# The MLP's second product by seven products of half-size blocks, in a hybrid decoder step on one core

## The chip, the cores and the metric

The kernel runs on one core of one Trainium2 chip. The metric is the device time of one execution in microseconds (us); lower is better. Engines are named as in the profile: PE does matmuls, PEld loads their stationary operands, DVE and ACT are the vector and the scalar engine, POOL is GpSimd, SP issues most transfers.

## The reference

One inference step of a one-layer decoder on 2048 prompt tokens (model width 1024) and 8 x 8 sample tokens: a shared input projection; forgetting attention (FoX) over the prompt and, for the sample tokens, over 8192 cached positions in pages; an mLSTM recurrence; an output projection with layer norm; and a squared-ReLU MLP with a second layer norm. All data are float32. The part that matters here is the end:

```python
mix = jnp.concatenate([fox_h, mn], axis=-1) @ w_o
x1 = _layer_norm(DN_ALPHA * x + mix, ln1_g, ln1_b)
hid = jnp.square(jax.nn.relu(x1 @ w1))             # 1024 -> 4096
return _layer_norm(DN_ALPHA * x1 + hid @ w2, ln2_g, ln2_b)   # 4096 -> 1024
```

## The kernel before

Each product of float32 operands is made of three matmuls on split operands: ACT rounds an operand to the matmul's reduced form ("hi", `split_hi`, L153), DVE subtracts that from the original ("lo", `split_lo`, L156), and `mm3` (L161 to L163) issues hi x hi, hi x lo and lo x hi into one PSUM bank.

The program has stages: the input projection with the mLSTM, the prompt attention (`phase_b`), the output projection with the first norm (`phase_o`), and the MLP (`phase_c`). The attention of the sample tokens over their cached pages is a Python generator of 294 steps. `tick(us)` counts the work that has been emitted and calls the next step (`attend`) each time `PACE_C` = 5 more has gone by in the last two stages. A step loads, scores or weighs: gathers of keys (`k_gather`, L1479, tile `kT`) and of values (`v_gather`, L1590, tiles `vt`, or `xr` and `vx` while `vx["more"]` allows a second place) are issued from POOL; `qk_step` (tile `sQ`) and `pv_step` (tile `sO`, L1614) are their matmuls. `take_back` runs steps until the second place is empty again.

`phase_c` goes over four blocks of tokens, `CB`: three of four tiles of 128, and a last one with the 64 sample rows added as tile 16 (576 columns). Within a block there are 16 groups of 256 hidden features:

- `hidden(fc)`: two weight tiles of `w1` (`piece`: one 512 KB load into `wr`, split into `wh` and `wl`), then for each 128 features a PSUM bank `ph` of 8 x 3 matmuls (moving operand 512 tokens wide, or twice 288 in the last block), Relu and Square on ACT into `hq`, and the split into `hh` and `hl`.
- `output([fc])`: two weight tiles of `w2`; for each token tile and each half of the 1024 output columns a bank `py` of 2 x 3 matmuls with 512 columns, which DVE adds into the row tile `y` (L1305; at the first group L1303 also multiplies by alpha). The last two groups share one call, `output([14, 15])`; after each tile's last addition there stands `layer_norm` (statistics, the power on POOL at L173, scaling on ACT at L175, gain on DVE at L176, bias on POOL at L177, or on DVE in the last block) and the store.

The order is `hidden(fc)`, then `output([fc - 1])`. Before the last `output` of a block, the next block's normed rows are loaded and turned by PE transposes into the operands `x1h` and `x1l` (`load`, `x1_turn`). In the third block, after group 13, the remaining attention steps are run, and `sampled()` does the output projection and first norm of the sample rows and stores them, to be read back as tile 16. The framework's scheduler orders each engine's instructions by the order of emission and a simulated readiness, so matmuls of `hidden` and `output` are found interleaved on PE.

## Time and profile before

| | |
|---|---|
| median of 3 runs | 3358.97 us (3357.42 to 3363.64) |
| the profiled execution | 3354.03 us; its span 3352.3 us, granted PE clock 0.986 |
| busy share of the span | PE 96%, DVE 56%, ACT 41%, POOL 26% |
| the MLP's first and last matmul | at 1607.0 us and 3338.2 us of the span |
| second-product matmuls | 3 x 1088 with 512 columns (of them 3 x 64 for the 64 sample rows) |

The span goes from the first to the last instruction on the core; the profiled execution's own time has 1.7 us around it. Times in rows of the trace count from the span's start. A group row gives the source line, engine, operation, output and input with their shapes, the number of instructions, their busy time, the mean duration of one in ns, and the idle time before them with what ended it. PE's matmuls overlap at their ends, so the distance between starts is the price of one, not its duration.

### The profile page before, as it was taken

The numbers are of one execution on the slowest core, as the hardware profiler recorded it, in microseconds if no ns is written. First come the engines' busy times: TensorE is split into PE (matmuls) and PEld (weight loads), VectorE is DVE, ScalarE is ACT, GpSimd is POOL, SyncE is SP. The second block draws the span as 40 slices with busy tenths as digits, with TensorE's granted clock in tenths as the row PEclk, the third lists the DMA queues.
The fourth block names the chain that finished last, engine by engine and source line by source line (L and its number), as shares of the span: only waits on it lengthen the run. The fifth ranks groups of instructions, "written<-read, shape, count | busy, mean of one in ns | idle before, by whom it ended". The sixth has DMA issues, their size and how long they took to land.

```text
span 3352.3 us, 58232 instructions
## 1 busy us (share of the span) xinstructions
PE 3225.8 (96%) x22065; PEld 2635.4 (79%) x22065; DVE 1890.9 (56%) x4781; ACT 1364.1 (41%) x2795; POOL 877.3 (26%) x925
## 2 busy tenths in 40 slices
PE   8999999998979999899999999999999999999998
PEld 8998998887857667677777777777777777888887
DVE  6857565455377878444544455445554545645545
ACT  4333343333278888422332333233433423433332
POOL 0031242332322222365322234323252110100000
PEclk9999999999989999999999999999999999999999
DMA  5575766767662322586876768767677554532221
GB/s 182 151 221 186 232 219 217 251 202 243 187 197 74 108 83 58 212 292 238 287 246 244 243 222 320 264 226 276 215 287 286 176 169 152 167 120 79 88 76 66
DMA packets 316000, 650.48 MB, mean 194 GB/s; under 512 B 61000, under 2 KB 175048, under 8 KB 314824
## 3 DMA queue, kind: packets, MB, share of 16 engines
q1 hardware_dynamic: 239032, 367.55, 35.1%
q0 software_dynamic: 74304, 270.57, 22.1%
q10 hardware_dynamic: 2384, 8.65, 0.7%
q8 instruction: 174, 2.85, 0.3%
q14 instruction: 106, 0.87, 0.1%
HBM read 593.82 MB, written 52.83 MB: 193 GB/s over the span
## 4 chain that ended last, share of the span: by engine, by line
PE 47%; DMA 4%; DVE 1%; POOL 1%; issue 1%; ACT 1%; SPq 0%; ACTq 0%; POOLq 0%; DVEq 0%
PE py L161 7%; PE py L162 7%; PE py L163 7%; PE ph L161 6%; PE ph L163 6%; PE ph L162 6%; PE sO L1614 3%; PE sQ L1502 2%; DMA wr<-w 2%; DMA vt<-cache_v,idxV 1%; PE sT L1571 1%; DMA kT<-cache_k,idxK 1%; DVE wl L156 0%; DMA vx<-cache_v,idxV 0%; PE pw L162 0%
## 5 line engine op out<-in xcount | busy, mean ns | idle before, releaser
L1305 DVE TENSOR_TENSOR y<-y,py 128x512 f32<-128x512 f32 (+1 forms) x476 | 326.2, 686 | 380.6 <-PE py L163 374.8
L153 ACT ACTIVATE wh<-wr 128x1024 fp32r<-128x1024 f32 x268 | 277.7, 1056 | 501.5 <-PE py L163 307.4
L161 PE MATMUL ph<-x1h,wh 128*128 128x512 f32 (+1 forms) x1280 | 455.1, 356 | 4.3 <-ACT wh L153 3.8
L162 PE MATMUL ph<-x1l,wh 128*128 128x512 f32 (+1 forms) x1280 | 453.6, 354 | 0.0
L163 PE MATMUL ph<-x1h,wl 128*128 128x512 f32 (+1 forms) x1280 | 451.4, 353 | 0.2 <-DVE wl L156 0.2
L161 PE MATMUL py<-wh,hh 128*128 128x512 f32 (+1 forms) x1088 | 432.6, 398 | 3.6 <-DVE y L1303 3.6
L1479 POOL DMA_INDIRECT kT<-cache_k,idxK x256 | 262.5, 1025 | 658.1 <-PE sQ L1502 596.0
L162 PE MATMUL py<-wl,hh 128*128 128x512 f32 (+1 forms) x1088 | 427.2, 393 | 0.7 <-DVE wl L156 0.7
L156 DVE TENSOR_TENSOR wl<-wr,wh 128x1024 fp32r<-128x1024 f32 x268 | 336.6, 1259 | 160.2 <-PE ph L163 82.1
L163 PE MATMUL py<-wh,hl 128*128 128x512 f32 (+1 forms) x1088 | 425.8, 392 | 0.0
L161 PE MATMUL pm<-xh,whi 128*128 128x256 f32 (+1 forms) x1024 | 302.4, 295 | 0.0
L162 PE MATMUL pm<-xl,whi 128*128 128x256 f32 (+1 forms) x1024 | 298.1, 291 | 0.0
L163 PE MATMUL pm<-xh,wlo 128*128 128x256 f32 (+1 forms) x1024 | 297.0, 290 | 0.0
L161 PEld LDWEIGHTS ph<-x1h,wh 128*128 128x128 f32 x1280 | 241.3, 189 | 45.7 <-issue 7.0
L163 PEld LDWEIGHTS ph<-x1h,wl 128*128 128x128 f32 x1280 | 241.2, 188 | 35.5 <-issue 2.1
L162 PEld LDWEIGHTS ph<-x1l,wh 128*128 128x128 f32 x1280 | 241.3, 188 | 34.6 <-issue 1.6
L161 PEld LDWEIGHTS py<-wh,hh 128*128 128x128 f32 (+1 forms) x1088 | 200.9, 185 | 60.6 <-issue 14.0
L161 PE MATMUL pm<-whi,xh 128*128 128x256 f32 (+2 forms) x816 | 237.6, 292 | 9.2 <-ACT whi L153 9.0
L1590 POOL DMA_INDIRECT vt<-cache_v,idxV x158 | 162.1, 1026 | 314.5 <-PE sO L1614 249.1
L163 PEld LDWEIGHTS py<-wh,hl 128*128 128x128 f32 (+1 forms) x1088 | 200.9, 185 | 49.5 <-issue 2.5
L162 PEld LDWEIGHTS py<-wl,hh 128*128 128x128 f32 (+1 forms) x1088 | 201.0, 185 | 41.6 <-issue 1.6
L162 PE MATMUL pm<-wlo,xh 128*128 128x256 f32 (+2 forms) x816 | 232.9, 286 | 0.6 <-DVE wlo L156 0.6
(349 smaller groups left out, 6549.8 us busy)
## 6 DMA issues: line engine op xcount, KB each, us to landing
wr<-w SPq DMA_DIRECT2D x256, 512.0 KB
wra<-w_in SPq DMA_DIRECT2D x104, 512.0 KB
Rb<-dR SPq DMA_DIRECT2D x128, 128.0 KB
xn<-xp_t SPq DMA_DIRECT2D x16, 512.0 KB
kn<-k_prompt SPq DMA_DIRECT2D x64, 128.0 KB
qn<-dq SPq DMA_DIRECT2D x128, 64.0 KB
wr<-w_o SPq DMA_DIRECT2D x16, 512.0 KB
xr<-dmix SPq DMA_DIRECT2D x16, 512.0 KB
```

The source lines that it names most:

```text
L153: last["ACT"] = A.activation(dst, src, AF.Copy, scale=scale)
L156: r = (eng or V).tensor_tensor(dst, src, hi.bitcast(F32), op=OP.subtract)
L161: T.matmul(ps, wh, xh, start=first, stop=False)
L162: T.matmul(ps, wh, xl, start=False, stop=False)
L163: last["PE"] = T.matmul(ps, wl, xh, start=False, stop=stop)
L1305: V.tensor_tensor(y, y, ps, op=OP.add)
L1479: G.indirect_dma_start(out=piece(n), out_offset=None, in_=ck, in_offset=IO(ap=idxK[:, b, j // 2, j % 2:j % 2 + 1], axis=0))
L1502: r = T.matmul(pq[h4 * 32:h4 * 32 + 32, hg].rearrange("p (k c) -> p k c", k=2), z["qb"][:, hd], kv, start=(db == 0), stop=(db == 1), skip_ ...
L1571: T.transpose(p[:, f], z["U"][u][:, hg, f].rearrange("p k t -> p (k t)"), ident)
L1590: G.indirect_dma_start(out=vt.rearrange("p f c -> p (f c)"), out_offset=None, in_=cv, in_offset=IO(ap=idxV[:, b, (kt % 4) * 4 + kt // 4, f ...
L1614: after_ = T.matmul(po[r:r + 32], z["PT"][:, hg, 2 * f + g, pg].rearrange("p h q -> p (h q)"), vts[f][:, g, hg * 256:(hg + 1) * 256], star ...
```

## The change

The 4096 hidden features are taken as two halves, and group `p` of the first half is worked together with group `p` of the second. One call of `output(p)` multiplies the block's four token tiles by 512 rows of `w2`. Both operands are cut in 2 x 2: tokens (two tiles each) by features (`a11`, `a12`, `a21`, `a22`), features by columns (`b11`, `b12`, `b21`, `b22`). In place of eight block products it does seven, in Winograd's variant of Strassen's form. Two of them are plain (a11 b11 and a12 b21, done first); the five others use sums of blocks, written in place: four of activations (`s`, `a21`, `a11`, `s` again) on DVE, four of weights (`b11`, `b12`, `b11`, `b11`) on POOL. Two PSUM banks (`X`) and two more (`Z`) go on accumulating after DVE has added their state so far into an output block, so there are 14 additions into `y` per call. Each of the seven operands is split only after its sum (`made`), two products ahead of its use. The 64 sample rows of the last block are multiplied plainly, beside those products whose weights fit (`extra`).

Around it: `hidden(p, half)` leaves its result unsplit in one of three `hq` tiles. `hidden(p + 1, 0)` is emitted before `output(p)` and `hidden(p + 1, 1)` after it. The host lays `w2` out by blocks. The next block's tokens are turned one by one between the products of the last `output`; two of their loads are issued before it. Norm statistics are taken per half row as soon as that half is complete (`norm_stats`), and in the last block the rest of the norm and the store go by halves on DVE (`norm_end`). Buffers: `wr` 5 for 4, `wh` 4 for 5, `hh` and `hl` 3 of [128, 2, 256] for 4 of 576 columns, `ph` 2 banks for 3, `py` 4 for 3; `jp` shares a buffer, and the scratch for POOL's transfer descriptors is set to 8192. Cut to its core:

```diff
-    def mm3(ps, wh, wl, xh, xl, first, stop):
+    def mm3(ps, wh, wl, xh, xl, first, stop, shared=False):
...
+    def norm_end(x, np_, st, g, b, wk, out, quick):
+        mv = wk.tile([128, 2], F32, name="ln_m2", bufs=2)
+        V.bn_aggr(mv[:np_], st[:np_])
+        rs = wk.tile([128, 3], F32, name="ln_r2", bufs=2)
+        V.tensor_scalar(rs[:np_, 0:1], mv[:np_, 1:2], EPS, None, op0=OP.add)
+        G.tensor_tensor(rs[:np_, 1:2], rs[:np_, 0:1], nhalf[:np_, 0:1], op=OP.pow)
+        if not quick:
...
+        h = [slice(i * 512, i * 512 + 512) for i in range(2)]
+        for i, e in ((0, SY), (1, A)):
+            V.scalar_tensor_tensor(x[:, h[i]], x[:, h[i]], mv[:np_, 0:1], g[:np_, h[i]], op0=OP.subtract, op1=OP.mult)
+        for i, e in ((0, SY), (1, A)):
+            V.scalar_tensor_tensor(x[:, h[i]], x[:, h[i]], rs[:np_, 1:2], b[:np_, h[i]], op0=OP.mult, op1=OP.add)
+            e.dma_start(out[:, h[i]], x[:, h[i]])
...
-        return pcw.tile([128, 1024], F32, name="wr", bufs=4)
+        return pcw.tile([128, 1024], F32, name="wr", bufs=5)
...
-        wh = C["pc"].tile([128, 1024], F32R, name="wh", bufs=5).rearrange("p (k c) -> p k c", k=k)
+        wh = C["pc"].tile([128, 1024], F32R, name="wh", bufs=4).rearrange("p (k c) -> p k c", k=k)
...
+            sums = {(0, 0): 2, (0, 1): 2, (1, 0): 1, (1, 1): 2, (2, 0): 2, (2, 1): 3}
...
+            def output(p, begun=None):
+                f1, f2 = H.pop((p, 0)), H.pop((p, 1))
+                a11, a21, a12, a22 = f1[:, :, 0:256], f1[:, :, 256:512], f2[:, :, 0:256], f2[:, :, 256:512]
+                b21, b22, b12, b11 = (raw() for _ in range(4))
+                for q, b in ((2, b21), (3, b22), (1, b12), (0, b11)):
+                    SY.dma_start(b, I["w2"][p, q])
+                s = ph.tile([128, 2, 256], F32, name="s", bufs=1)
...
+                def made(n):
+                    v = lambda o, x, y, op: V.tensor_tensor(o, x, y, op=op)
+                    g = lambda o, x, y: G.tensor_tensor(o, x, y, op=OP.subtract)
+                    w = lambda b: piece(None, b.rearrange("p (k c) -> p k c", k=2))
+                    if n == 1:
+                        r = split(a12), w(b21)
+                    elif n == 0:
+                        v(s, a21, a22, OP.add)
+                        r = split(a11), w(b11)
+                        v(a21, a11, a21, OP.subtract)
+                        v(a11, s, a11, OP.subtract)
+                        g(b11, b12, b11)
+                        g(b12, b22, b12)
+                    elif n == 2:
+                        r = split(s), w(b11)
+                        v(s, a12, a11, OP.subtract)
+                        g(b11, b22, b11)
+                    elif n == 3:
+                        r = split(a11), w(b11)
+                        g(b11, b21, b11)
+                    else:
+                        r = (split((s, a21, a22)[n - 4]), w((b22, b12, b11)[n - 4]))
+                    return r
...
+                plan = [(0, "X", True, False, 0, 0), (1, "Y", True, True, 0, 0), (3, "X", False, False, 0, 1), (2, "Z", True, False, 2, 1),
+                        (4, "Z", False, True, 0, 1), (5, "X", False, False, 2, 1), (6, "X", False, True, 2, 0)]
+                extra = {0: (0, (0, 1)), 1: (1, (0,)), 2: (0, (1,)), 4: (1, (1,))}
+                for at_, (n, kind, first_, last_, r0, half) in enumerate(plan):
+                    if at_ + 2 < 7:
+                        ops.append(made(at_ + 2))
+                    (h, l), (wh, wl) = ops[n]
+                    for i in range(2):
...
+                        for k in range(2):
+                            mm3(ps, h[:, k, c], l[:, k, c], wh[:, k], wl[:, k], first_ and k == 0, last_ and k == 1, True)
+                        add(blk[r0 + i], half, ps)
+                        tick(1.28)
...
+                    if begun and at_ in (0, 1, 3, 4):
+                        turn(ci + 1, (0, 1, 3, 4).index(at_), begun)
...
+            hidden(0, 0)
+            hidden(0, 1)
+            for p in range(8):
+                if p < 7:
+                    hidden(p + 1, 0)
+                if p == 6:
                     vx["more"] = None
...
+                output(p, begun if p == 7 and ci < 3 else None)
+                if p == 6 and ci < 3:
                     take_back()
+                    begun = [x1_load(t) for t in CB[ci + 1][:2]]
+                if p < 7:
+                    hidden(p + 1, 1)
+                if p == 6 and ci == 2:
                     while acc[1] is not None:
                         tick(100.0)
                     sampled()
```

## The prediction

> **What bounds the kernel now.** I read the page's busy shares first, then busy time by stretch of the second half (the MLP runs from about 1607 us to the end), then PE's instructions in order of time, PE's waits, and last DVE's and POOL's groups.

> ```profile
> span 3352.3 us, 58232 instructions
> PE 3225.8 (96%) x22065; PEld 2635.4 (79%) x22065; DVE 1890.9 (56%) x4781; ACT 1364.1 (41%) x2795; POOL 877.3 (26%) x925
> core 0: us, PE busy (x) PEld busy (x) DVE busy (x) ACT busy (x) POOL busy (x), PEclk, DMA share, GB/s
> 2060.00:2445.00 385.00, 379.16 (x2414) 286.72 (x2412) 185.14 (x382) 128.32 (x216) 128.53 (x129) 1.00 0.71 255
> 2890.00:2915.00 25.00, 24.82 (x128) 20.11 (x127) 19.39 (x34) 8.63 (x12) 7.31 (x5) 1.00 0.28 102
> 2915.00:2960.00 45.00, 43.97 (x286) 40.30 (x286) 26.59 (x36) 21.90 (x38) 6.37 (x4) 1.00 0.60 205
> 2960.00:3300.00 340.00, 340.00 (x2009) 301.84 (x2009) 169.77 (x231) 116.86 (x206) 0.00 (x0) 1.00 0.27 81
> PE py L161 <- DVE y L1303: 3.2, 1, 3.2
> PE sO L1614 <- DMA vt<-cache_v,idxV: 1.8, 1, 1.8
> PE sQ L1502 <- DMA kT<-cache_k,idxK: 0.8, 1, 0.8
> ```

> In the second block of tokens (2060 to 2445) PE is busy 379.16 of 385 us at full clock; its three waits there make up the 5.8 that are missing. In the last block (2960 to 3300) it never idles. DVE is at 48 to 50%, ACT at 33 to 34%, POOL at 33% and then nothing. So this stage lasts as long as its matmuls, and a matmul taken out of it is worth its own pitch, as long as the three other engines still deliver in time. A busy PE is not by itself proof of matmuls at full rate, so the pitch comes from the order of time: the first and the last of twelve consecutive second-product matmuls (128x512), nothing between them.

> ```profile
> L161 PE MATMUL py<-wh,hh 128*128 128x512 f32 x1024 | 407.7, 399 | 3.6 <-DVE y L1303 3.6
> 2460.28 0.39 PE L161 MATMUL py<-wh,hh 128*128 128x512 f32 x1
> ...
> 2462.78 0.39 PE L163 MATMUL py<-wh,hl 128*128 128x512 f32 x1
> ```

> Eleven steps in 2.50 us are 0.2273 us each. The group row's 399 ns is the time of one with its drain, which the next one overlaps; it is not the price.

> **The matmuls removed.** Before, two feature groups (a "pair" from here on) cost, per block of four token tiles, 2 groups x 4 tiles x 2 halves x 2 contraction steps x 3 = 96 matmuls. The new `output(p)` has seven products x 2 tiles x 2 x 3 = 84. The 64 sample rows of the last block cost 24 per pair either way (`extra` has four entries of six). So 12 go per pair, 8 pairs x 4 blocks = 32 pairs: 384, an eighth of the 3072 that the row's x1024 times three forms gives. 384 x 0.2273 = 87.3 us off PE. The first product is untouched.

> **What is added, engine by engine.**

> ```profile
> L1305 DVE TENSOR_TENSOR y<-y,py 128x512 f32<-128x512 f32 x103 | 70.6, 686 | 85.8 <-PE py L163 85.1
> L156 DVE TENSOR_TENSOR wl<-wr,wh 128x1024 fp32r<-128x1024 f32 x55 | 67.2, 1224 | 42.6 <-PE ph L163 25.3 <-PE py L162 5.2 <-issue 5.1
> L156 DVE TENSOR_TENSOR hl<-hq,hh 128x512 fp32r<-128x512 f32 x30 | 21.3, 710 | 32.3 <-ACT hh L153 32.3
> L153 ACT ACTIVATE wh<-wr 128x1024 fp32r<-128x1024 f32 x56 | 58.0, 1056 | 151.6 <-PE py L163 108.4 <-PE ph L162 23.4 <-DMA wr<-w 18.7
> L153 ACT ACTIVATE hh<-hq 128x512 fp32r<-128x512 f32 x30 | 18.9, 630 | 5.3 <-PE py L162 4.6
> L177 POOL TENSOR_TENSOR y<-y,b 128x1024 f32<-128x1024 f32 x28 | 68.1, 2431 | 52.7 <-DVE y L176 43.9 <-DVE ln_rs L172 8.6
> ```

> Weight splits per pair go from 8 to 11 (four for the first product, then 4 becomes 7), activation splits from 4 to 7, four sums of activations appear on DVE (two SBUF operands of 512, so I price them by the hl row), and the additions into y fall from 16 to 14. DVE per pair: before 8 x 1.224 + 4 x 0.710 + 16 x 0.686 = 23.6 us; after 11 x 1.224 + 11 x 0.710 + 14 x 0.686 = 30.9, so 7.3 more. ACT: 3 x 1.056 + 3 x 0.630 = 5.1 more. POOL: four subtractions of 128x1024, by the L177 row 4 x 2.43 = 9.7 more. The window of 385 us holds seven pairs (55 weight splits, 8 per pair), so a pair lasts 55 us with DVE at 26.4, ACT at 18.3 and POOL at 18.4. After: 52.3 us with DVE 33.7, ACT 23.4, POOL 28.1. On average all three stay below PE and the additions cost nothing. The DMA loads are as many and as large as before.

> **Where the averages hide something.** The added work is not spread evenly: the weight-split buffers fall to four, two of which hold the first product's pieces until that ends, so of the seven operand pairs only two are fully split when the seven products start. Inside their 84 x 0.2273 = 19.1 us DVE then has 5 x 1.224 + 4 x 0.710 + one sum of 0.710 + 14 x 0.686 = 19.3 us. That is even, with no allowance for POOL, and here POOL matters:

> ```profile
> 2911.18 2.41 POOL L177 TENSOR_TENSOR y<-y,b 128x1024 f32<-128x1024 f32 x1 [3.94 <-DVE ln_rs L172]
> 2912.00 2.67 DVE L156 TENSOR_TENSOR wl<-wr,wh 128x1024 fp32r<-128x1024 f32 x1
> 2915.20 1.20 DVE L156 TENSOR_TENSOR wl<-wr,wh 128x1024 fp32r<-128x1024 f32 x1
> 2919.74 2.40 POOL L177 TENSOR_TENSOR y<-y,b 128x1024 f32<-128x1024 f32 x1 [4.66 <-DVE ln_rs L172]
> 2920.12 4.25 DVE L156 TENSOR_TENSOR wl<-wr,wh 128x1024 fp32r<-128x1024 f32 x2 [0.39 <-ACT wh L153]
> ```

> A split that starts while a POOL addition runs takes 2.67 instead of 1.20 us: it ends 1.08 us after POOL's end at 2913.59. The two splits under the other POOL addition take 4.25, some 1.85 more than two. So one such POOL operation costs DVE 1.5 to 1.9 us if a split meets it, and each pair now has four. The additions into y have one operand in PSUM. [...]

> What this costs PE I take from the stretch where such meetings happen now, 2890 to 2960, with four POOL additions: PE lost 0.18 + 1.03 = 1.2 us, 0.3 per operation. Two of a pair's four subtractions (b22-b11 and b21-b11) fall into the seven products, the other two under the first product's matmuls. 2 x 0.3 x 32 = **19 us**. Bounds: nothing, if first-product matmuls fill each gap (the scheduler interleaves the two kinds already); and two full meetings per pair, 2 x 1.85 x 32 = 118 us. Below nothing it can't go: the last block had no idle time to win.

> PSUM waits are in the same price: a bank that is added from and then accumulated further (the products 2 then 4, 5 then 6) must be read before its next matmul.

> ```profile
> 3291.41 0.39 PE L163 MATMUL py<-wh,hl 128*128 128x512 f32 x1
> 3291.84 0.69 DVE L1305 TENSOR_TENSOR y<-y,py 128x512 f32<-128x512 f32 x1 [2.13 <-PE py L163]
> ```

> DVE is through 1.12 us after the last matmul's start, and the other tile's six matmuls cover 7 x 0.2273 = 1.59; one 1.2 us split ahead of it in DVE's queue already uses that up.

> **Block seams.** The transposes of the next tokens now lie between the last products rather than before them, with the norms of the block. The last `output` has 14 additions instead of 8, 14 splits more or less at once, and the same norm work, while its cover falls from 96 to 84 matmuls. Before, a seam costs almost nothing (0.18 us of 25 above at the third). I take 2 us for each of three, **6 us**; bounds -2 (the 3.2 us wait at a block's first addition can go, since three first-product groups now run ahead of it) and 30, half an `output` uncovered at each. The token loads move along: two are issued before the last first-product group, the others after each turn, on SP's queue behind four weight loads that wait for buffers; the y rows are all asked for at the first `output` on ACT's queue, 33 us into the block instead of 22. Both have that lead as cover and cost nothing; without it a load would be late by the few us that it takes, which the 30 holds. The fourth instead of fifth wh buffer at the entry to the MLP lies in that.

> **End of the sample attention and its rows.**

> ```profile
> L1634 DVE TENSOR_REDUCE mixs<-sT x64: 148/168/180, 806.6 to 2827.2; 64x8 f32<-64x16 f32 x64
> 2866.23 0.48 SPq L1247 DMA_DIRECT2D dx<-y  x1
> 2893.47 5.04 SPq L1097 DMA_DIRECT2D xr<-dx  x2
> L1479 POOL DMA_INDIRECT kT<-cache_k,idxK x256 | 262.5, 1025 | 658.1 <-PE sQ L1502 596.0 <-issue 54.0 <-PE sO L1614 2.2
> ```

> The attention's steps are paced by `tick`. By the code, through the point in the third block where the rest is flushed, the old order gives 2 x 327.7 + 27 x 10.24 = 932 us of ticks, the new one 2 x 307.2 + 163.8 + 7 x 17.9 = 903, at 5 per step six steps fewer. Before, the last step ended at 2827, and it took 39 us until the sample rows were stored (2866) and 66 until they were being loaded back. Now some steps pile up at the flush, and between it and the use of the rows lie one `output` of 19 us, the rows' own product and the first quarter of the next first product. POOL's subtractions also wait for the splits of the tile they overwrite, and the gathers (and the norms' powers) queue behind them, for which PE's sO waits. I take **5 us** for all of that, with 0 and 25 (39 us less 19 and a few) as bounds. The smaller descriptor scratch I take at nothing: the gathers' idle time is put down to PE, which frees their tiles, and the rest is the usual 0.2 us of issue each, with no sign of a full ring. The moved `jp` tile costs one wait at the very start, before anything of this.

> **The end.**

> ```profile
> 3338.22 0.40 PE L163 MATMUL py<-wh,hl 128*64 128x512 f32 x1
> 3338.84 0.68 DVE L168 BATCH_NORM_STATS2 ln_st<-y 64x6 f32<-64x512 f32 x1
> ...
> 3346.75 1.22 DVE L177 TENSOR_TENSOR y<-y,b 64x1024 f32<-64x1024 f32 x1
> 3338.00:3353.00 15.00, 0.62 (x3) 0.13 (x1) 7.42 (x12) 2.48 (x2) 1.22 (x2) 0.60 0.25 87
> ```

> From the end of the last matmul (3338.6) to DVE's last is 9.4 us, and 4.3 more to the span's end. Now both last tiles are full ones finished by DVE alone: after the last matmul about 0.3 + eleven operations of 0.68 to 0.69 (the two tiles' remaining addition, statistics and four half passes each, less what fits before) + small ones, some 8 us, and the same 4.3. **-1.5 us**, bounds -4 and +2.

> **Sum.** -87.3 + 19 + 6 + 5 - 1.5 = -58.8 us. The profiled execution took 3354.03 (span 3352.3 and 1.7 around it): 3295 for it. The median of the runs is 3358.97, 4.9 above; the same difference taken from it gives **3300**.

> **Rivals.**

> *Full gain:* the scheduler fills all gaps with first-product matmuls as in the last block now; the three added costs stay under 12 us in all. 3359 - 87 - 1.5 + 0 to 12 = 3270 to 3283. For it: DVE's average of 64%. Against: the even balance inside the products.

> *Late sample rows or seams:* seams at 10 us and the sample chain at 25 give 3359 - 87 + 19 + 30 + 25 - 1.5 = 3344. For it: the 39 us chain above with half the cover. Against: the next first product can start on tiles that don't need these rows.

> *DVE and POOL bind the products (slower):* the weights of product 3, the third in order, are made from b11 in a chain: ACT 1.056, DVE 1.224, POOL 2.43, ACT 1.056, DVE 1.224 = 7.0 us, counted from the release of the first product's first weight piece, twelve matmuls before its end; cover is 36 x 0.2273 = 8.2. Slack is 1.2 us, and one met lock (1.85) or a pair of gathers ahead on POOL eats it. It decides from 87.3 / 32 = 2.73 us of stall per pair. With both meetings in full, 3.7 per pair: 118 us in place of 19, so 3399. For it: the rows of 2911 and 2920, and the sum 33.7 + 9.7 = 43.4 of 52.3 us. Against: that sum is still below PE, and PE lost only 0.3 us per operation where it happens now. [...]

> **How the numbers follow.** Between runs of this kernel about 0.2% can be told from no change, so same is 3352 to 3366. Chances: forecast (3283 to 3325) 0.56; full gain 0.16; late rows or seams (3325 to 3350) 0.13; DVE and POOL bind, 0.15, of which 0.03 end within 0.2%. Faster 0.85, same 0.03, slower 0.12. The range 3268 to 3345 takes in the first three almost whole and leaves out about 0.18.

> **What would show it.** Right: 896 matmuls of each py form at 128x512 for full tiles, unchanged pitch, DVE about 64% busy in the second block, wl splits with a mean clearly above 1224 ns, PE idle in the MLP up by some 30 us, most of it before py matmuls with DVE wl or y as releasers, and sO waits little changed. Wrong: PE idle of 2.7 us or more per pair (the slower rival), a gap of over 10 us around the third seam, or PE idle no larger than now (full gain).

## The result and the profile after

The changed kernel takes 3369.3 us (median) against 3357.7 for the kernel before; the ratio is 1.0039, with a 95% interval of 1.0025 to 1.0053. It is slower by 0.4%, where 1.8% faster was forecast. The profiled execution of the changed kernel took 3387.5 us, 18 above its median and the slowest of its 18 runs; that of the kernel before took 3354.0, 4 below its own. So 33 us lie between the two traces where 12 lie between the medians, and the losses read from the trace below are larger than the usual ones.

The page's busy shares, changed kernel:

```profile
span 3385.8 us, 57876 instructions
PE 3181.0 (94%) x21681; PEld 2578.7 (76%) x21681; DVE 2263.1 (67%) x5067; ACT 1503.1 (44%) x2966; POOL 1252.5 (37%) x1053
```

The 384 matmuls are gone (22065 to 21681), yet PE's busy time fell by 44.8 us, not by 87.3, and its idle time (span less busy) rose from 126.5 to 204.8. Two more columns tell where. Busy time by stretch, the kernel before first, then the changed one; each from the MLP's first matmul, the fourth row up to the start of the last block, the fifth the last block. The first number behind the comma is PE's busy time; the number behind the last bracket is the granted TensorE clock, as a share of full speed.

```profile
1607.00:2007.00 400.00, 395.59 (x2474) 300.37 (x2475) 192.79 (x386) 135.55 (x223) 121.77 (x130) 0.99 0.72 248
2007.00:2407.00 400.00, 391.69 (x2517) 296.06 (x2516) 201.20 (x404) 139.71 (x227) 145.59 (x140) 1.00 0.75 271
2407.00:2807.00 400.00, 395.68 (x2326) 299.23 (x2326) 202.78 (x360) 139.62 (x221) 99.49 (x94) 1.00 0.62 216
2807.00:2920.00 113.00, 110.81 (x583) 92.00 (x582) 75.58 (x113) 43.95 (x56) 10.60 (x8) 1.00 0.45 149
2920.00:3338.00 418.00, 416.97 (x2452) 368.42 (x2451) 218.87 (x302) 147.58 (x258) 8.99 (x7) 1.00 0.29 90
```

```profile
1603.00:2003.00 400.00, 386.15 (x2367) 288.86 (x2365) 272.74 (x433) 170.16 (x266) 211.14 (x153) 0.99 0.72 245
2003.00:2403.00 400.00, 369.51 (x2274) 273.26 (x2275) 272.71 (x447) 160.36 (x245) 207.39 (x155) 0.97 0.70 251
2403.00:2803.00 400.00, 380.82 (x2257) 283.07 (x2256) 278.85 (x441) 175.03 (x277) 190.31 (x133) 0.97 0.62 217
2803.00:2958.00 155.00, 131.95 (x712) 103.41 (x711) 110.92 (x147) 63.04 (x84) 40.22 (x24) 0.92 0.50 163
2958.00:3366.00 408.00, 399.81 (x2360) 351.21 (x2359) 319.36 (x364) 181.00 (x288) 109.23 (x40) 0.99 0.28 90
```

In the first three blocks PE idled 19.2 us before (four rows: length less busy) and 86.6 after: 67 more. The clock adds to that. Length times what is missing from a clock of 1.00 is some 5 us before (the 0.99) and 40 after (4 + 12 + 12 + 12.4 by the rows); by the trace's record of the clock 33 of the 40 fall into time in which PE works, and 5 before, so 28 more. The other 7 lie inside PE's idle time and are counted there already. Against the 24 x 2.73 = 65.5 us of matmuls saved there, 67 and 28 make a net loss of about 30. The three blocks in fact became 41.2 us longer: their first matmul comes 3.6 us earlier (1603.45 against 1607.01), the last block's first ReLU 37.6 us later (2957.85 against 2920.25). Some 11 us are left over. About 6 of them are the ends of matmuls, which nothing overlaps when PE stops: 0.39 less 0.23 us at each of 38 more stops. The rest is not explained. The last block got shorter, 418.0 to 408.2 us, where 21.8 were to be had. The stretch behind the last matmul grew from 14.1 to 19.7.

PE's waits in the MLP of the changed kernel (total, times, longest):

```profile
PE sO L1720 <- DMA vt<-cache_v,idxV: 21.0, 9, 6.0
PE py L163 <- DVE hl L156: 14.4, 8, 2.4
PE py L161 <- DVE y L1306: 14.0, 9, 3.2
PE py L161 <- ACT wh L153: 11.8, 2, 10.6
PE py L161 <- ACT hh L153: 5.7, 3, 3.8
PE sO L1720 <- DMA xr<-cache_v,idxV: 5.3, 2, 3.2
```

Three kinds stand there: the attention's gathers come late (26.3 us for vt and xr, 6.2 before), the operands of the seven products come late from DVE and ACT, and there is one wait of 10.6 us at the third seam (a seam is a block's end, from its last pair to the next block), behind the sample rows. That one has a chain of its own (SPq is SP's queue, which issues the loads):

```profile
2917.94 1.22 DVE L176 TENSOR_TENSOR y<-y,g 64x1024 f32<-64x1024 f32 x1 [1.31 <-ACT y L175]
2919.18 0.33 SPq L1324 DMA_DIRECT2D wr<-w  x1
2922.73 2.00 ACT L153 ACTIVATE wh<-wr 128x1024 fp32r<-128x1024 f32 x2 [4.83 <-DMA wr<-w]
2923.84 0.79 PE L161 MATMUL py<-wh,hh 128*128 128x512 f32 x1 [10.64 <-ACT wh L153]
```

By the code the sample rows' norm keeps its gain and bias vectors in two of the five `wr` buffers. The last output loads `b11` last, though its first product needs it, and that load is issued only when DVE's multiplication by the gain has freed a buffer. So PE waits here for a buffer and a transfer, not for splits or additions that DVE is too slow for.

What this kernel's longest sO wait did to the clock is seen in stretches of 2 us around the 6.03 us wait of an sO at the first seam:

```profile
2034.00:2036.00 2.00, 1.37 (x18) 0.52 (x16) 2.00 (x6) 1.05 (x1) 0.74 (x1) 1.00 1.01 313
2036.00:2038.00 2.00, 0.00 (x0) 0.00 (x0) 2.00 (x5) 0.00 (x0) 1.15 (x2) 0.94 1.02 416
2038.00:2040.00 2.00, 0.00 (x0) 0.00 (x0) 0.49 (x2) 0.00 (x0) 0.00 (x0) 0.50 1.03 410
2040.00:2042.00 2.00, 0.60 (x8) 0.37 (x12) 0.00 (x0) 0.00 (x0) 0.00 (x0) 0.50 1.04 424
2042.00:2044.00 2.00, 2.00 (x27) 0.84 (x22) 0.00 (x0) 0.00 (x0) 0.95 (x1) 0.50 1.02 418
2044.00:2046.00 2.00, 2.00 (x15) 1.18 (x9) 1.06 (x10) 0.00 (x0) 1.66 (x2) 0.85 1.03 418
```

PE stops at 2035.4 and resumes at 2041.4, but at a clock of 0.50 until about 2044.6 (0.85 of a 2 us stretch). The wait costs its 6 us and some 1.6 more.

### The profile page after: what moved, and what is told of

Read it like the earlier page. It is cut to its first block, busy times and chain, and to the rows that moved or that the text cites. A ratio compares the mean times of both kernels' runs of the same rounds, so it can differ in the third digit from the quotient of the medians.

```text
span 3385.8 us, 57876 instructions
## 1 busy us (share of the span) xinstructions
PE 3181.0 (94%) x21681; PEld 2578.7 (76%) x21681; DVE 2263.1 (67%) x5067; ACT 1503.1 (44%) x2966; POOL 1252.5 (37%) x1053
## 4 chain that ended last, share of the span: by engine, by line
PE 30%; issue 7%; DVE 6%; DMA 6%; POOL 5%; ACT 1%; POOLq 0%; SPq 0%; DVEq 0%; ACTq 0%
PE ph L161 5%; PE ph L162 5%; PE ph L163 5%; PE py L161 4%; PE py L163 3%; PE py L162 3%; DMA vt<-cache_v,idxV 3%; POOL wr L1353 2%; DVE wl L156 2%; PE sO L1720 2%; PE sQ L1608 1%; DMA wr<-w 1%; DVE y L1306 1%; POOL kT L1585 1%; POOL vt L1696 1%
## 5 line engine op out<-in xcount | busy, mean ns | idle before, releaser
L156 DVE TENSOR_TENSOR wl<-wr,wh 128x1024 fp32r<-128x1024 f32 x364 | 504.2, 1391 | 232.7 <-ACT wh L153 231.8
L153 ACT ACTIVATE wh<-wr 128x1024 fp32r<-128x1024 f32 x364 | 380.0, 1054 | 396.4 <-PE py L163 165.4
L1353 POOL TENSOR_TENSOR wr<-wr 128x1024 f32<-128x1024 f32 x128 | 341.1, 2665 | 470.4 <-DVE wl L156 447.5
L161 PE MATMUL ph<-x1h,wh 128*128 128x512 f32 (+1 forms) x1280 | 456.4, 357 | 4.1 <-ACT hq L1293 3.9
L162 PE MATMUL ph<-x1l,wh 128*128 128x512 f32 (+1 forms) x1280 | 454.2, 355 | 0.0
L163 PE MATMUL ph<-x1h,wl 128*128 128x512 f32 (+1 forms) x1280 | 453.1, 355 | 0.0
L1585 POOL DMA_INDIRECT kT<-cache_k,idxK x256 | 280.7, 1097 | 410.3 <-PE sQ L1608 326.3
L161 PE MATMUL py<-wh,hh 128*128 128x512 f32 x896 | 358.8, 408 | 31.7 <-DVE y L1306 14.0
L163 PE MATMUL py<-wh,hl 128*128 128x512 f32 x896 | 350.7, 401 | 14.4 <-DVE hl L156 14.4
L162 PE MATMUL py<-wl,hh 128*128 128x512 f32 x896 | 357.0, 399 | 1.3 <-DVE wl L156 1.3
L1306 DVE TENSOR_TENSOR y<-y,py 128x512 f32<-128x512 f32 x416 | 276.6, 679 | 94.4 <-PE py L163 92.5
L161 PE MATMUL pm<-xh,whi 128*128 128x256 f32 (+1 forms) x1024 | 302.2, 295 | 0.0
L162 PE MATMUL pm<-xl,whi 128*128 128x256 f32 (+1 forms) x1024 | 297.7, 291 | 0.0
L163 PE MATMUL pm<-xh,wlo 128*128 128x256 f32 (+1 forms) x1024 | 296.7, 290 | 0.0
L161 PEld LDWEIGHTS ph<-x1h,wh 128*128 128x128 f32 x1280 | 242.1, 189 | 44.3 <-ACT hq L1293 6.0
L163 PEld LDWEIGHTS ph<-x1h,wl 128*128 128x128 f32 x1280 | 241.8, 189 | 36.3 <-issue 5.0
L162 PEld LDWEIGHTS ph<-x1l,wh 128*128 128x128 f32 x1280 | 241.8, 189 | 34.7 <-issue 4.1
L161 PE MATMUL pm<-whi,xh 128*128 128x256 f32 (+2 forms) x816 | 237.5, 292 | 8.7 <-ACT whi L153 8.7
L161 PEld LDWEIGHTS py<-wh,hh 128*128 128x128 f32 x896 | 171.7, 193 | 87.1 <-ACT wh L153 24.0
L162 PE MATMUL pm<-wlo,xh 128*128 128x256 f32 (+2 forms) x816 | 233.2, 286 | 0.6 <-DVE wlo L156 0.6
L163 PE MATMUL pm<-whi,xl 128*128 128x256 f32 (+2 forms) x816 | 232.9, 285 | 0.0
```

Of the source, the lines that this page charges most:

```text
L153: last["ACT"] = A.activation(dst, src, AF.Copy, scale=scale)
L156: r = (eng or V).tensor_tensor(dst, src, hi.bitcast(F32), op=OP.subtract)
L161: T.matmul(ps, wh, xh, start=first, stop=False, skip_group_check=shared)
L162: T.matmul(ps, wh, xl, start=False, stop=False, skip_group_check=shared)
L163: last["PE"] = T.matmul(ps, wl, xh, start=False, stop=stop, skip_group_check=shared)
L1306: V.tensor_tensor(y, y, ps, op=OP.add)
```

## The experiments

Three theories stood at first: POOL (the weight subtractions there), SEAM (the last output of a block, with no first products beside it), ORDER (what else moved). Ratios are to the kernel before, run on the same chip; 0.001 is 3.4 us.

**The last output plain** (`flat7`). A branch at the head of `output` gives `p == 7` the old form:

```
if p in flat:            # flat = {7}: both halves of the contraction in one PSUM tile
    ...                  # per token tile and half: mm3 over 2 k x 2 j, one add
    return
...
if p == 7 and ci < 3:    # turns ahead of the last output
    for i in range(len(CB[ci + 1])):
        turn(ci + 1, i, begun)
```

The branch also loads the four weight blocks in the order `b11`, `b12`, `b21`, `b22`.

> Edit to the changed kernel: the last output of each of the four blocks (pair 7) is done by plain products again, with both k-halves of a pair fused into one accumulation (96 matmuls, eight additions), without subtractions or sums of weights and activations, and the next block's tokens are turned ahead of it, as before the change. The other 28 outputs keep the seven products. Theory SEAM (the loss sits in the last output of each block, which has no first products beside it and so hangs on the vector engine): the remainders of the blocks (first ReLU of the last pair to first ReLU of the next block, 95.0, 95.6 and 114.5 us in the changed kernel against 77.6, 82.3 and 54.7 before) fall to about 80, 82 and 100, the end after the last product by 4 to 8 us; less 4 x 2.7 us of matmuls won back by the plain form, so 35 to 45 us below the changed kernel, ratio to the kernel before about 0.99. Theory POOL (the four weight subtractions of a pair on the POOL engine, its lock with the vector engine and the gathers behind them, cost inside every pair): one eighth of it goes, 5 us, against 11 us of matmuls back: within 10 us of the changed kernel, ratio 1.002 to 1.007. Theory ORDER (the new order around the products, not the products' form, costs): no change beyond the 11 us of matmuls, ratio 1.007.

Measured: 0.989 (0.9873 to 0.9906), 50 us below the changed kernel, though 11 us of matmuls came back. In the profiles the last block starts at 2924.9 instead of 2957.9, and the end behind the last matmul is 13.0 instead of 19.7 us. SEAM holds as to the place, and larger than it expected. Why the loss sits there this run does not say: the edit takes away the last output's sums, splits, additions and POOL subtractions together, and changes its load order.

**All outputs plain** (`flat_all`): the same branch for every p, the halves of the contraction one after the other.

> Edit to the changed kernel: all 32 outputs by plain products (96 matmuls each and 16 additions, in the shape they had before), with the next block's tokens turned ahead of a block's last output; what stays of the change is everything else: the padded or shared buffers, sample rows behind pair 6 of the third block, norms by halves, and the end of the last block. Theories SEAM and POOL: the rest of the change is nearly free, so within 10 us of the kernel before (3348 to 3370), ratio 0.997 to 1.003. Theory ORDER: the rest carries the loss, which the seven products only partly pay for: 3358 + 60 to 100 us, ratio 1.018 to 1.03.

Measured: 1.0051 (1.0034 to 1.0067). That is not ORDER's 60 to 100 us, nor nothing. The edit differs from the old shape in one point: before, the last output of a block summed both halves in PSUM. With that too as it was (`flat_all_f7`, `flat = {0..6: two steps, 7: one}`):

> Edit to the changed kernel: all outputs by plain products as in flat_all (ratio 1.0051), but the last of each block with both k-halves of the pair in one accumulation (96 matmuls, eight additions), as the kernel before had it. In flat_all the four norms of a block come in one bunch near its end, and POOL's share of them (two additions of 4.67 us in one row) stands ahead of the attention's gathers; here a token tile is finished every 24 matmuls. If this bunch at the seams is what the rest of the change costs: 0.997 to 1.001. If it is smaller buffers or the order inside the pairs: 1.003 to 1.006.

Measured: 0.9994 (0.9981 to 1.0007). So with plain products the rest of the change costs nothing, and ORDER falls. Even with plain products, eight more additions and norms that end in a bunch in the last output of each block cost 19 us. POOL's queue in `flat_all` shows one such place; PE's next sQ waited 6.11 us for the gather that stands behind the two additions:

```profile
2060.19 1.44 POOL L1728 DMA_INDIRECT vt<-cache_v,idxV  x1 [0.30 <-issue]
2061.64 4.67 POOL L193 TENSOR_TENSOR y<-y,b 128x1024 f32<-128x1024 f32 x2
2066.47 0.96 POOL L1617 DMA_INDIRECT kT<-cache_k,idxK  x1 [0.16 <-issue]
```

How the 19 us divide between the additions and the bunch is open.

**The subtractions left out** (`no_sub`: `g = lambda o, x, y: None`), **moved to DVE** (`sub_dve`: `V.tensor_tensor` in place of `G.tensor_tensor`), **made small** (`sub_small`: on `[:, 0:32]`).

> Edit to the changed kernel: the 128 subtractions of weights on POOL are left out (the products are formed with the unsubtracted weights, so the output is not the reference's); matmuls, splits, additions, loads and their order stay. Theory POOL: the lock and the gathers behind the subtractions go everywhere, the MLP's PE waits on vt, wl, hl and y fall by half or more, 30 to 40 us less than the changed kernel, ratio to before 0.992 to 0.995; the split of a weight (wl) falls from 1391 to about 1280 ns mean. Theory SEAM: only the seams' POOL pairs go, 3 to 4 us each with no first products beside them, 10 to 15 us, ratio about 1.000. Theory ORDER: less than 8 us, ratio 1.002 to 1.004.

> Edit to the changed kernel: the four weight subtractions of a pair are issued on the vector engine in place of POOL, at the same places in the order of the program; nothing else. At the pace of a wl split without a lock (about 1.2 us for 128x1024) they add 4 x 1.2 x 32 = 154 us to DVE's 2263 us. Theory POOL (lock and head-of-line blocking on POOL dominate): faster than the changed kernel by 10 to 25 us inside the blocks, where DVE has room (26.4 + 7.3 + 4.8 = 38.5 of 52 us a pair), less some 4.8 us at each seam. Theory SEAM (DVE is what binds the last output of a block): the four seams and the end lose 3 to 5 us each, the pairs win little: 5 us faster to 20 us slower than the changed kernel. Theory ORDER: no change within 8 us.

> Edit to the changed kernel: each of the 128 subtractions on POOL works on 32 of its 1024 columns only (so the output is not the reference's); every instruction, its place in the queues and every wait stay, only the time that POOL spends in it falls from 2.4 us to a few tenths. It splits what leaving the subtractions out gained (ratio 0.9842 against 1.0039). Theory LOCK (POOL's long operations hold back DVE's splits and sums while they run, and the gathers behind them): most of it comes back, ratio 0.985 to 0.990. Theory CHAIN (the waits that a subtraction brings: gathers and the norms' powers queued on POOL behind one that waits for a DVE split, and the chain ACT, DVE, POOL, ACT, DVE behind product 3): most of the loss stays, ratio 0.997 to 1.003.

Measured: 0.9842 (0.9823 to 0.9861), 0.9908 (0.9891 to 0.9925) and 0.9869 (0.9849 to 0.9889): 66, 44 and 57 us below the changed kernel. The subtractions cost far more than expected: 57 of the 66 us by their length, at most some 9 by the waits and the chain that they bring (the intervals of `no_sub` and `sub_small` overlap). The trace of `sub_small` shows where: PE's waits for DVE's `hl` and `y` in the MLP fall from 28.4 to 4.5 us, those of sO for the gathers from 26.3 to 12.5. The wait of 10.6 us at the third seam stays: it is 10.5 to 10.8 us in the profiles of `no_sub`, `sub_small`, `sub_dve` and, further below, `sub_mix` and `turn_first`, and 13.3 in `sub_memset`. In `flat7` no wait of a py matmul for `wh` is longer than 2.0 us. Moving them to DVE, with its 67%, wins 44 us. DVE's groups say why, first the changed kernel, then `sub_small` (busy us, mean ns of one):

```profile
L156 DVE TENSOR_TENSOR wl<-wr,wh 128x1024 fp32r<-128x1024 f32 x357 | 494.1, 1389 | 232.7 <-ACT wh L153 231.8 <-issue 0.4
L156 DVE TENSOR_TENSOR hl<-hq,hh 128x512 fp32r<-128x512 f32 x160 | 150.0, 937 | 42.3 <-ACT hh L153 42.3
L1352 DVE TENSOR_TENSOR s<-hq 128x512 f32<-128x512 f32 x64 | 84.8, 1325 | 12.1 <-ACT hq L1294 11.1
L156 DVE TENSOR_TENSOR hl<-s,hh 128x512 fp32r<-128x512 f32 x64 | 79.7, 1245 | 0.0
L1353 POOL TENSOR_TENSOR wr<-wr 128x1024 f32<-128x1024 f32 x128 | 341.1, 2665 | 470.4 <-DVE wl L156 447.5 <-issue 14.8 <-DMA wr<-w 4.2
```

```profile
PE 3166.1 (95%) x21681; PEld 2572.4 (77%) x21681; DVE 2087.6 (63%) x5067; ACT 1499.5 (45%) x2966; POOL 947.0 (28%) x1053
L156 DVE TENSOR_TENSOR wl<-wr,wh 128x1024 fp32r<-128x1024 f32 x358 | 443.1, 1241 | 291.2 <-ACT wh L153 252.4 <-issue 33.7 <-PE py L163 4.2
L156 DVE TENSOR_TENSOR hl<-hq,hh 128x512 fp32r<-128x512 f32 x160 | 114.1, 713 | 57.0 <-ACT hh L153 56.7
L1352 DVE TENSOR_TENSOR s<-hq 128x512 f32<-128x512 f32 x64 | 44.6, 697 | 16.4 <-ACT hq L1294 15.4
L156 DVE TENSOR_TENSOR hl<-s,hh 128x512 fp32r<-128x512 f32 x64 | 43.9, 686 | 0.3 <-ACT hh L153 0.3
```

The same DVE instructions take 2263.1 us beside POOL's long subtractions and 2087.6 beside the short ones: 175 us, 1.4 us for each of the 128. The sums and their splits, which stand in DVE's queue right where POOL works, take almost twice as long. `sub_dve` shows the comparison that matters:

```profile
PE 3168.8 (95%) x21681; PEld 2573.0 (77%) x21681; DVE 2229.4 (67%) x5195; ACT 1501.7 (45%) x2966; POOL 907.4 (27%) x925
L1353 DVE TENSOR_TENSOR wr<-wr 128x1024 f32<-128x1024 f32 x128 | 156.2, 1220 | 1.6
```

Doing the subtractions itself costs DVE 142 us (2229.4 less 2087.6), less than the 175 it loses when POOL does them.

**POOL's reading, or POOL's time** (`sub_memset`: three `G.memset(o, 0.0)` for each subtraction), **and the subtractions beside plain products** (`plain_dummy`: in `flat_all_f7`, `G.tensor_tensor(o, x, o, op=OP.subtract)` on weight tiles that are done with, 112 in all).

> Edit to the changed kernel: each of the 128 subtractions on POOL is replaced by three fills of the same 128x1024 tile with zeros, which read nothing (so the output is not the reference's). By the profile's fills of 32 and 4 columns (123 and 105 ns, 0.65 ns a column) three take about 2.3 us, so POOL is held as long as by a subtraction (2.43 undisturbed) and waits for the same splits. Theory LOCK (DVE's operations with two SBUF operands are held back while POOL reads): ratio like the small subtractions, 0.985 to 0.990, wl back near 1.25 us mean. Theory GATHERS (POOL's time delays the gathers, for which PE waits): like the changed kernel, 1.000 to 1.004.

> Edit to flat_all_f7 (all outputs plain, ratio 0.9994): in each pair but the last of a block, four subtractions of 128x1024 run on POOL on the weight tiles after their splits have read them (112 in all; nothing uses the results). Theory LOCK: DVE has room here (56 per cent busy) and loses 112 x 1.5 to 1.9 us at most, so PE loses little: 0.999 to 1.003. Theory GATHERS: POOL's 112 x 2.4 us stand ahead of the same gathers as in the changed kernel, PE's waits for vt, xr and kT rise by 20 us and more in the first three blocks: 1.008 to 1.015, with nothing in the fourth block.

Measured: 0.9915 (0.9897 to 0.9933) and 0.9985 (0.9972 to 0.9998). `sub_memset`:

```profile
PE 3168.0 (95%) x21681; PEld 2569.8 (77%) x21681; DVE 2086.1 (63%) x5067; ACT 1499.8 (45%) x2966; POOL 1258.1 (38%) x1309
L156 DVE TENSOR_TENSOR wl<-wr,wh 128x1024 fp32r<-128x1024 f32 x356 | 437.4, 1235 | 300.5 <-ACT wh L153 270.3 <-issue 24.6 <-PE ph L163 5.3
L1353 POOL MEMSET wr<- 128x1024 f32 x384 | 367.5, 957 | 590.7 <-DVE wl L156 345.7 <-DMA wr<-w 130.1 <-DVE y L1306 50.7
```

POOL is held even a little longer (367.5 us against 341.1), yet DVE's time is that of `sub_small` (2086.1 us against 2087.6): what holds DVE back is not POOL being busy. The subtractions, which read two SBUF tiles, do it; the fills, which read none, do not. Nor does it meet all of DVE's instructions: wl, hl and the sums, with two SBUF operands, take longer in the rows above, while the 416 additions `y<-y,py`, with one operand in PSUM, take 679 ns in the changed kernel and 680 in `sub_small`. Of the 57 us that the small subtractions give back, the fills give 42 (1.0039 to 0.9915); the last 15 (0.9915 against 0.9869, intervals apart) go with POOL's time as such. `plain_dummy` looks at it from the other side: 278 us of subtractions on POOL (2482 ns each), with the same gathers, cost a kernel nothing whose DVE has room (1922.7 us busy, 57%). But they also meet less of DVE's work there: DVE loses 48 us to them (1875.0 in `flat_all_f7`), 0.4 us each and not 1.4. LOCK holds. That it costs only where DVE is short of time fits both runs; no run has the full 175 us on a DVE with room.

**Which two of the four** (`sub_mix`: b22 less and b21 less on DVE, the other two on POOL).

> Edit to the changed kernel: of a pair's four weight subtractions the two that fall between the seven products (b22 less the first difference, b21 less the second) go to DVE; the two beside the first product's matmuls stay on POOL. If the place decides, as the prediction had it (only the two inside the products cost): nearly all of what moving all four to DVE gave (ratio 0.9908 against 1.0039), 0.988 to 0.993. If every POOL subtraction costs the same wherever it lies: half of it, 0.996 to 0.999. If the first two cost more, since the gathers of the attention queue behind them: 0.999 to 1.003.

Measured: 0.9957 (0.9942 to 0.9971). 27 of the 44 us come from the two inside the products, 17 from the two beside the first product. Taken away in this order, each pair of them costs, the inner one more.

**The sample rows earlier** (`early`: `if p == 5 and ci == 2` for 6, `PACE_C = 4.65`), and the same with plain products.

> Edit to the changed kernel: the sample rows' product (and the flush of the sample attention ahead of it) stands behind pair 5 of the third block instead of pair 6, and the attention's pace is 4.65 instead of 5 ticks per step, so that it is through by there. Theory SEAM-3 (the third block's end is longer by 20 to 40 us because the rows' product, its w_o loads on SP's queue ahead of the last output's weights, and the last output without first products fall together): third remainder from 114.5 to about 90, 15 to 25 us faster than the changed kernel, ratio 0.996 to 1.000. Rival (the faster pace makes PE wait for the gathers, which POOL issues late between its subtractions): the pairs of the first three blocks lose what the seam wins, 1.001 to 1.006.

> Edit to the changed kernel: all outputs by plain products (as in flat_all, ratio 1.0051) and the sample rows behind pair 5 with the pace of 4.65. If the place of the sample rows is what the rest of the change costs: ratio 0.998 to 1.001, the third remainder back from 87 to about 70. If it is something else (buffers, the end by halves, the order of the two halves of a pair): 1.004 to 1.007.

Measured: 0.9984 (0.9973 to 0.9995), 18 us below the changed kernel, and 1.0057 (1.0037 to 1.0078), no change against `flat_all`. Each run changes two things, the place and the pace. In the profile of `flat_all_early` the third remainder (first ReLU of a block's last pair to the first ReLU of the next block) falls (87.1 to 74.6 us) while the first rises (79.7 to 92.2), so the earlier place helps with plain products too and something else, most likely the faster pace, takes it back. Neither the place nor the pace was run by itself.

**The turns alone** (`turn_first`: the loop over `turn` ahead of `output(7)`, which keeps its seven products).

> Edit to the changed kernel: the next block's tokens are turned ahead of a block's last output, as before the change, not between its products; the last output keeps the seven products and POOL keeps the subtractions. If the turns between the last products make the seams' loss: half or more of flat7's gain (ratio 0.989 against 1.0039), 0.992 to 0.997. If it is the seven products' own load on DVE with no first products beside them: 1.001 to 1.006.

Measured: 1.0064 (1.0039 to 1.0089): nothing won. `flat7` gains by the plain form.

**Both, and variations of both** (`flat7_dve`, `flat7_mix`; `flat7_dve_early`; `flat7_dve_quick`: `norm_end(..., True)`).

> Edit to the changed kernel: the last output of each block by plain products (as in the run flat7) and the weight subtractions of the other 28 on DVE (as in sub_dve). If the two losses are apart (the seams from DVE's work, the inside of the blocks from POOL's), they add: 0.989 + 0.9908 - 1.0039 = 0.976, 3285. If they are one loss, met at the seams (POOL's subtractions under the last outputs), then no better than the better of the two, 0.987 to 0.990. In between, 0.980 to 0.985, if about half of it is shared.

> Edit to the changed kernel: the last output of each block plain (as in flat7) and of the other 28 outputs' subtractions the two inside the products on DVE, the two beside the first product's matmuls on POOL. If DVE's own time inside a pair is what flat7_dve (0.9834) still pays: 0.980 to 0.983. If any POOL subtraction costs more than it saves on DVE: 0.985 to 0.988.

> Edit: the run flat7_dve (last output plain, subtractions on DVE, ratio 0.9834) and the sample rows behind pair 5 with the pace of 4.65. If the third seam is a loss by itself: its remainder falls from 102 to some 80, and 10 to 18 us of the 18 that the same step gave alone remain, 0.978 to 0.981. If the plain last output has taken it already: 0.982 to 0.986.

> Edit: the run flat7_dve with the norms of all blocks in the form of the last one (four half passes on DVE, nothing of 2.4 us on POOL or 1 us on ACT). If POOL's norm additions ahead of the gathers cost PE at the three seams: 5 to 12 us less than flat7_dve, 0.980 to 0.982. If DVE is what the seams lack: its 12 x 1.6 = 19 us more come in part onto the path, 0.984 to 0.987.

Measured: `flat7_dve` 0.9834 (0.9817 to 0.9852), `flat7_mix` 0.985 (0.9826 to 0.9874), `flat7_dve_early` 0.9877 (0.9856 to 0.9898), `flat7_dve_quick` 0.9857 (0.9839 to 0.9874). The two remedies give 50 and 44 us alone and 69 together, so some 25 us were one loss, most likely POOL's subtractions under the last outputs. With the seam plain, moving the sample rows together with the faster pace costs 14 us, more than either theory had: the third remainder does fall as the first of them said (102.0 to 79.7 us in the profiles), and the first two rise (83.7 to 92.1, 87.8 to 92.0). `flat7_dve` is 1.7% faster than the kernel before, and 2.0% faster than the changed one by the two ratios; `flat7_mix` and `flat7_dve_quick` can't be told from it. Of the 28 x 2.73 = 76 us that its matmuls save it keeps 56.

## Why the prediction was wrong, step by step

**-87.3 us of matmuls: right.** Successive pairs of the last block, by the first ReLU of two of them, changed kernel and then `sub_dve`:

```profile
3225.42 0.41 ACT L1293 ACTIVATE hq<-ph 128x288 f32<-128x288 f32 x1 [0.25 <-PE ph L163]
3276.07 0.41 ACT L1293 ACTIVATE hq<-ph 128x288 f32<-128x288 f32 x1 [0.25 <-PE ph L163]
```

```profile
3227.46 0.41 ACT L1293 ACTIVATE hq<-ph 128x288 f32<-128x288 f32 x1 [0.92 <-PE ph L163]
3277.56 0.41 ACT L1293 ACTIVATE hq<-ph 128x288 f32<-128x288 f32 x1 [0.92 <-PE ph L163]
```

A pair takes 50.10 us without POOL's subtractions; before it took 52.9. That is 2.8, against 2.73 forecast. Twelve matmuls taken out were worth their pitch there, as the prediction had it.

**"On average all three stay below PE and the additions cost nothing": the step that failed.** The change itself adds 197 us to DVE (1890.9 to 2087.6; 7.3 x 32 = 234 were forecast). But the 175 us lost to POOL's reads were left out of the average, though the prediction quoted the rows that show them. With them DVE is at 68% of the second block's stretch above (272.71 of 400) and at 78% of the last (319.36 of 408). That is still below PE, as the slower rival's sum of 43.4 of 52.3 us was (it counts POOL's subtractions at their full 2.43 us; no run shows that, 1.4 us were lost for each). So the average was too low, and, what matters more, an average below PE did not mean that PE never waits: the waits come at single places, where a split, a sum or an addition is late for the next matmul (28.4 us for `hl` and `y` in the changed kernel, 4.5 in `sub_small`).

**+19 us for DVE and POOL: mis-sized.** The runs put it at 57 (`sub_small`). In the last block, where nothing of the attention runs, the size comes out: pairs take 50.65 instead of 50.10 us, 0.55 against the 0.6 forecast. But that is luck, for it is not the two subtractions that were priced. `sub_mix`, which has those two on DVE, still takes 50.63:

```profile
3211.36 0.39 ACT L1293 ACTIVATE hq<-ph 128x288 f32<-128x288 f32 x1
3261.99 0.39 ACT L1293 ACTIVATE hq<-ph 128x288 f32<-128x288 f32 x1
```

So there the two beside the first product's matmuls cost the 0.55 us, which the prediction took as free. The price of 0.3 us was also taken over to the first three blocks, where the attention's steps and gathers share DVE and POOL; most of the 57 us lies there and at the seams.

**+6 us for the seams, bounds -2 to 30: wrong.** The 2 us for each were taken from a seam that cost almost nothing before; the 30 were "half an `output` uncovered". `flat7` gets 50 us back after paying 11 for matmuls; with the subtractions on DVE it is still 25 and 11 (0.9908 to 0.9834), so 36, of which some 5 are the shorter end. The likely reason is that no first-product matmuls stand beside the last output, while splits, 14 additions and four norms all come onto DVE there; the turns are not it (`turn_first`). At the third seam the wait of 10.6 us for a `wr` buffer, shown above, is part of it, and the prediction had not looked for it. Put into the sum, 57 and 36 give -87.3 + 93 = about +6 us, where 13 were measured (0.0039 of 3358); they come from different surroundings and need not add exactly.

**+5 us for the sample rows, bounds 0 to 25: mis-sized, within its bounds.** `early` gives 18, for the earlier place and the faster pace together, and it goes together with the seam's loss. The gap of over 10 us at the third seam that was to show the forecast wrong is there (10.6).

**-1.5 us at the end: wrong, +5.6.** It took two tiles' halves to be left behind the last matmul. In fact all five tiles' norms end there. The changed kernel's last matmul and the first and last of DVE's half passes:

```profile
3366.07 0.39 PE L163 MATMUL py<-wh,hl 128*128 128x512 f32 x1
3366.96 1.40 DVE L198 SCALAR_TENSOR_TENSOR y<-y,ln_m,g 128x512 f32<-128x512 f32 x2
...
3381.11 1.41 DVE L200 SCALAR_TENSOR_TENSOR y<-y,ln_r,b 128x512 f32<-128x512 f32 x2
```

In `flat7`, whose tiles end one after another, 13.0 us follow the last matmul, and 14.1 in the kernel before.

**The clock was missing from the sum.** Every stall was priced at its own length. The 28 us of lower clock while PE works, in the first three blocks, come on top of 67 us of idle time, 0.4 us for each.

**What was to show it.** 896 matmuls of each form, an unchanged price and a wl mean above 1224 ns (1389) came as said. PE's idle time rose by some 75 us in the MLP (86.6 + 8.2 less 19.2 and 1.0), 2.3 a pair, and not by 30, and sO's waits, which were to change little, went from 6 to 26 us. Of the rivals none came true alone: "late sample rows or seams" named two of the places and came at about its price (36 and 18 us against 30 and 25), "DVE and POOL bind" named the mechanism and came at about half (57 against 118). They were given chances as if only one could come; they can come together, for the seams and the products draw on the same DVE, and some 25 us belong to both. Not all of it is DVE: the 10.6 us at the third seam are not, and 12.5 us of sO's waits (6.2 before the change) stay when the subtractions are small.

## What to carry to other kernels

Work given to POOL was not free for DVE here: each of the 128 subtractions cost it 1.4 us. Add to DVE's account what its instructions with two SBUF operands lose beside POOL's reads, and compare it with doing the work on DVE (here 175 against 142 us). Where a change takes work off the bounding engine and puts it on others, look for the places where the bounding engine's independent work runs out, such as the last output of a block, and leave the old form there; four of 32 in the old form gave 50 us. Where PE stood still for 1.86 us or more of one 3.41 us window, the clock fell to 0.50 in the next (one window of 1.87 us excepted, below): price such a stop at more than its length (here 28 us on top of 67). And look where the buffers of the first load behind a side job come free: here two small vectors in a weight buffer held PE for 10.6 us.

## What the hardware showed beyond expectation

```profile
2478.08:2481.49 3.41, 1.43 (x9) 1.02 (x10) 3.41 (x8) 2.00 (x4) 1.03 (x1) 1.00 1.00 311
2481.49:2484.90 3.41, 3.41 (x9) 2.53 (x10) 3.41 (x6) 0.44 (x2) 0.00 (x0) 0.50 0.82 287
2157.22:2160.63 3.41, 1.54 (x7) 0.94 (x5) 3.41 (x3) 1.75 (x3) 2.95 (x3) 1.00 1.03 390
2160.63:2164.04 3.41, 2.75 (x11) 1.98 (x12) 3.41 (x6) 0.77 (x1) 0.84 (x1) 1.00 0.88 302
```

In the first PE idles 1.98 of 3.41 us, in two stops, and the clock is at 0.50 in the next; in the third it idles 1.87 and the clock stays. Every fall in the changed kernel's MLP follows a window with 1.86 to 3.41 us of idle time, and the most idle window without a fall behind it is the third row. So in this trace 1.86 us of idle time in a window of 3.41, somewhat more than half, could be enough, and 1.87 once was not; in the first row two stops add up to the 1.98.

POOL's memset of 128x1024 took 957 ns in `sub_memset`, where 0.65 ns per column and a start, from the profile's small fills (123 ns for 32 columns, 105 for 4), had given 0.77 us. The subtractions on POOL took 2665 ns beside the seven products, where DVE is busy for 2263.1 us, and 2482 in `plain_dummy`, where it is busy for 1922.7; no run takes the difference apart.
